# Where a pair's split weights begin in their tile: byte 88 in place of byte 8

## The chip, the cores and the metric

The kernel runs on one core of a Trainium2 chip. Its metric is the device time of one execution in microseconds. Five engines work side by side: TensorE multiplies matrices (PE in the profile; PEld is its load of the stationary operand, which overlaps the matmuls), VectorE (DVE), ScalarE (ACT) and GpSimd (POOL) work on elements, and SyncE (SP) only starts transfers. Operands of TensorE lie in SBUF, 128 partitions with a run of bytes in each; results go to PSUM.

## What is computed

A trunk of two encoder layers on 512 frames of 1024 channels, in float32. Each layer has two recurrent branches behind one wide projection, a merge, a channel block and an embedding:

```python
h = rmsnorm(x, norm1_g[i])
z = h @ w_in[i] + b_in[i]
...
y_m = (jax.nn.sigmoid(mo.astype(f32)) * head_layernorm(hm, m_norm_g[i], M_HEADS)).astype(dt)
...
y_r = (jax.nn.silu(rg.astype(f32)) * head_layernorm(hr, r_norm_g[i], R_HEADS)).astype(dt)
merged = jax.nn.sigmoid(gm) * (y_m @ w_bm[i]) + jax.nn.sigmoid(gr) * (y_r @ w_br[i])
x = x + merged @ w_out[i]
h2 = rmsnorm(x, norm2_g[i])
x = x + jnp.square(jax.nn.relu(h2 @ w_ff1[i] + b_ff1[i])) @ w_ff2[i] + b_ff2[i]
h3 = rmsnorm(x, norm3_g[i])
x = x + jax.nn.sigmoid(h3 @ w_pe_gate[i]) * (p[i] @ w_pe[i])
```

Nearly all of the time goes into the products with the weight matrices.

## The kernel before

**Three products for one.** TensorE works here on float32 values that are rounded to a shorter form (`F32R`). To keep the precision, every operand is split into a high part (rounded) and a low part (the rest), and a product becomes three matmuls: high by high, high by low, low by high (`mm3`, lines 488 to 490). Activations stay in SBUF in split form. Weights arrive from memory in raw tiles (`wr`), and `prep_next` splits each raw tile into a tile `both` with `split`: ScalarE writes the high half (line 309), VectorE the low half behind it (line 310). `both` has 2w + 64 float32 per partition, where w is 1024, or 512 for the piece called D.

**Units.** The work is a fixed list of units, in the order in which TensorE runs them. The kinds that matter here:

- `T8`: one column of 128 outputs by 1024 inputs. `t8` runs 24 matmuls; the weights are stationary (128x128) and the activations move, 512 columns.
- `PAIR`: two such columns together, by a scheme that needs seven products of half-size blocks in place of eight. `run_pair` runs seven products of 12 matmuls (lines 539 to 541), again with weights stationary and activations moving, now 256 columns. The weights of a pair lie in four tiles, `w_A`, `w_B`, `w_C` (two products each) and `w_D` (one).
- `WIDE`: the same scheme for values and gates, with activations stationary and weights moving (lines 583 to 585).
- The last four `T8` units (`LAST`) have tiles in a pool of their own and run with 256 columns at a time.

Besides these, `scores` and `attend` compute the recurrences in blocks, through `mm3` as well. In `attend` the split scores `ph` and `pl` are stationary and the split values `vh` and `vl` move; in branch A there are 258 columns, which start at column (h % 2) x 258 of the value tile for head h.

**Order.** Weights are prepared two pieces ahead of TensorE (`LOOK`), loads run on SyncE's queue in the order of the units with four raw tiles at a time, and `in_order` keeps splits and loads in that order. Sums of weight blocks that the seven-product scheme needs are made in memory by transfers on GpSimd's queue, at a pace set by the matmuls (line 367).

**Where operands start.** Tiles are placed one after another in a partition, and `o` in `prep_next` shifts the split weights inside their tile: by 2 float32 (8 bytes) for pairs and for the last four units, by none for the others. The two halves start at `o` and `o + w`; stationary blocks are 128 float32 (512 bytes) long, moving blocks 256 or 512 float32.

Of the kernel before, what the change touches and what calls it, by code (L numbers as in the profile page):

```python
# [124 lines left out]
def is_wide(g):  # L125
    return g[1][:2] in ("rv", "rw")
# [7 lines left out]
def has_t2(g):  # L134

    return is_full(g) or g[1][0] == "f"
# [117 lines left out]
def build(ctx, tc, ins, out):  # L254
    nc = tc.nc
    ve, ac, gp, te = nc.vector, nc.scalar, nc.gpsimd, nc.tensor
    units = [u for i in range(L) for u in unit_list(i)]
    NU = len(units)

    def pool(name, bufs, **kw):  # L260
        return ctx.enter_context(tc.tile_pool(name=name, bufs=bufs, **kw))
# [8 lines left out]
    wpool = pool("w", PIECES)  # L270
# [31 lines left out]
    def ps(name):  # L302
        return psum.tile([P, T], F32, name=name, tag="ps")
# [4 lines left out]
    def split(src, hi_ap, lo_ap):  # L308
        a = ac.activation(hi_ap, src, AF.Copy)  # L309
        return a, ve.tensor_sub(lo_ap, src, hi_ap.bitcast(F32))  # L310

    def in_order(kind, *new):

        for a, b in zip(cur.get(kind, ()), new):
            tc.add_manual_dep(b.ins, a.ins.name, ORDER, reason="order of the weights")
        cur[kind] = new
# [4 lines left out]
    for g, v in groups().items():  # L321
        index[g] = len(index)
        src, n, w = ("wwide", 2, UN) if is_wide(g) else ("wpairs", len(v), Q)
# [63 lines left out]
    def full(n):  # L387
        return units[n][0] in ("PAIR", "WIDE") and is_full(units[n][1])
# [10 lines left out]
    def halves(n):  # L399

        return [slice(0, Q), slice(Q, UN)] if n == 1 else [slice(0, UN)]

    def fill_raws(most=RAWS + 1):
        while at["load"] < len(loads) and len(raws) + len(kept) < most:
            n, x = loads[at["load"]]
            r = None
            if n in cur["room"] and cur["more"] not in raws:
                cur["more"] = n, x
                r = cur["low"].tile([P, UN], F32, name=f"wr{at['load']}", tag="wrx", bufs=1)
            elif len(raws) - (cur["more"] in raws) >= RAWS:  # L410
                break
            raws[n, x] = r = r or wpool.tile([P, UN], F32, name=f"wr{at['load']}", tag="wr", bufs=RAWS)
            if x:
                _, g, p = units[n]
                assert made.get((g, x[1] if is_wide(g) else p)) == 2 * len(MADE_OF(g)), (g, p, made, at["unit"])
                if is_wide(g):
                    in_order("load", nc.sync.dma_start(r, block(g, x[0])[x[1]]))
                else:
                    for k, y in enumerate(PIECE[x][:1] if x == "B" and not has_t2(g) else PIECE[x]):
                        in_order("load", nc.sync.dma_start(r[:, k * Q:(k + 1) * Q], block(g, y)[p]))  # L420
            elif units[n][0] == "IF":
                eng = nc.sync if n else nc.scalar
                eng.dma_start(r[:, 0:64], ins["wif"][n * L // NU])
            else:
                w = ins["wstream"][at["whole"]]
                for c in halves(n):
                    in_order("load", nc.sync.dma_start(r[:, c], w[:, c]))
                at["whole"] += 1
            at["load"] += 1

    def prep_next():
        n, x = order[at["prep"]]
        at["prep"] += 1
        fill_raws()

        w = Q if x == "D" else UN
        pl = cur["last"] if n >= NU - LAST else wpool
        kw = {"tag": "d", "bufs": 1} if x == "D" else {"tag": "l", "bufs": LAST} if pl is not wpool else {
            "tag": "w", "bufs": PIECES}
        wide = isinstance(x, tuple)  # L440
        nm = f"{x[0]}{x[1]}" if wide else x
        gates = units[n][0] == "IF"
        both = pl.tile([P, 2 * w + SLACK], F32R, name=f"w{n}_{nm}", **kw)
        o = 2 if units[n][0] == "PAIR" or pl is not wpool else 0
        out_ = [both[:, o + a * w:o + a * w + w] for a in range(1 if gates else 2)]
        r = formed.pop((n, x), None)
        if r is None:
            r = raws.pop((n, x))
        if gates:
            z = out_[0]  # L450
            gp.memset(z.bitcast(F32), 0.0)
            z = z.rearrange("p (k g c) -> p k g c", g=4, c=32)
            split(r[:, 0:64].rearrange("p (k g c) -> p k g c", g=2, c=H), z[:, :, 0:2, 0:H], z[:, :, 2:4, 0:H])
        elif x == 0:
            with tc.high_priority(AHEAD if n < 10 and units[n][0] == "V" or units[n][1:] == SOON else 0):
                for c in halves(n):
                    in_order("prep", *split(r[:, c], *[a[:, c] for a in out_]))
        else:
            in_order("prep", *split(r[:, :w], *out_))
        pieces[n, x] = out_  # L460
        if full(n) or not wide and x in ("A", "C") and has_t2(units[n][1]):
            pass
        elif x == "A" or wide and x[0] == "t2":
            kept[n, x] = r
        elif x == "C":

            ve.tensor_tensor(raws[n, "B"][:, Q:], kept.pop((n, "A"))[:, Q:], r[:, :Q], OP.add)
        elif x == "B":

            ve.tensor_tensor(r[:, :Q], r[:, :Q], r[:, Q:], OP.add)  # L470
            formed[n, "D"] = r
        elif wide and x[0] == "B21":
            t = cur["br"].tile([P, UN], F32, name=f"t4{n}_{x[1]}", tag=("ph", "pl")[x[1]])
            ve.tensor_tensor(t, kept.pop((n, ("t2", x[1]))), r, OP.add)
            formed[n, ("t4", x[1])] = t

    def ready(k):
        while at["prep"] < min(len(order), k + 1):
            prep_next()
# [12 lines left out]
    def t8(act, name):  # L492

        _, wh, wl = unit("T8")
        o = ps(name)
        for k in range(KT):
            s = slice(k * P, (k + 1) * P)
            mm3(o, wh[:, s], wl[:, s], act[0][k], act[1][k], k == 0, k == KT - 1)
            if k == 3:
                flush()  # L500
            if k in (2, 5):
                pace()
        return o
# [482 lines left out]
    for i in range(L):  # L986
# [322 lines left out]
        for d in range(4):  # L1309
            o = t8(xa, f"l{i}m0z{d}") if d else oz  # L1310
# [115 lines left out]
        for c in range(KT):  # L1426
# [6 lines left out]
            o = t8(yr, f"l{i}br1{c}")  # L1433
# [37 lines left out]
        for c in range(KT):  # L1471
            o = t8((mh, ml), f"l{i}wo{c}")
# [144 lines left out]
        for c in range(KT - LAST if last else KT):  # L1617
            o = t8(n3.act, f"l{i}pg{c}")
# [44 lines left out]
    for a, n in enumerate(nn):  # L1663
        for c in range(KT - LAST, KT):
            _, wh, wl = ws[c - KT + LAST]
            o = ps(f"pl{a}{c}")[:, :256]
# [141 lines left out]
```

## Time and profile before

| | |
|---|---|
| runs shown | 2291.69, 2293.63 and 2295.32 us, median 2293.63 |
| profiled execution | 2292.93 us, its span 2291.2 us |
| mean granted TensorE clock | 0.998 |
| instructions | 36395, of them 13532 matmuls |
| memory read and written | 478.03 MB and 194.51 MB |

The span runs from the first to the last instruction; the rest of an execution's time lies around it. A row of the timeline gives start, duration, engine, line, operation, the tiles as out<-in, and partitions x elements of the operand that moves. Ends of matmuls are modelled, and neighbours overlap, so what a matmul costs in a stream of them is the step from one start to the next. Names leave out buffer numbers: `l0r0brqa<-l0xnh,w_A` is a matmul from a pair's tile A and the high activations into the PSUM tile `a`.

### The profile page before, as it was taken

Reading aid. Unit: us, or ns where it says so; the run is one execution under the profiler, and the core shown is the slowest. Engines: PE = TensorE matmul, PEld = TensorE weight load, DVE = VectorE, ACT = ScalarE, POOL = GpSimd, SP = SyncE. Lnnn points to the kernel's source line nnn. Section 1 sums busy time; section 2 is a strip of 40 time slices with the busy share of each in tenths; the row PEclk is TensorE's granted clock in tenths of the full one; section 3 lists DMA queues with packets and bytes.
Section 4 is the critical chain, followed back from the end, with each engine's and each line's share of the span. In section 5 each row is a group of like instructions: output and inputs, shape, how many; then the busy total and the mean of one; then the engine's idle time right before and its main releaser. Section 6 shows DMA issues by size and latency. Waiting matters only on the chain.

```text
span 2291.2 us, 36395 instructions
## 1 busy us (share of the span) xinstructions
PE 2273.9 (99%) x13532; PEld 2019.5 (88%) x13532; DVE 1761.7 (77%) x2722; ACT 1266.5 (55%) x1835; POOL 607.7 (27%) x952
## 2 busy tenths in 40 slices
PE   9999999999999999999999999999999999999998
PEld 7888899888898899999888888988888988999997
DVE  7877767886767878778778787778868678787785
ACT  6756544654554546556557564445545546566564
POOL 3332222223124322223432332221221242111112
PEclk9999999999999999999999999999999999999999
DMA  6776887787788888888786768877877898878751
GB/s 215 192 191 174 244 232 218 216 236 220 220 247 260 216 230 234 232 245 214 222 225 184 195 178 250 235 215 223 229 217 214 248 263 221 247 236 230 229 161 56
DMA packets 187890, 499.33 MB, mean 218 GB/s; under 512 B 26352, under 2 KB 29808, under 8 KB 187712
## 3 DMA queue, kind: packets, MB, share of 16 engines
q0 software_dynamic: 57520, 188.53, 36.7%
q1 hardware_dynamic: 114496, 280.97, 36.3%
q10 hardware_dynamic: 15696, 27.50, 3.6%
q8 instruction: 106, 1.74, 0.3%
q14 instruction: 72, 0.59, 0.1%
HBM read 478.03 MB, written 194.51 MB: 294 GB/s over the span
## 4 chain that ended last, share of the span: by engine, by line
PE 88%; DVE 6%; ACT 2%; issue 2%; DMA 2%; POOL 0%; DVEq 0%; SPq 0%; ACTq 0%; POOLq 0%
PE l0f L488 1%; PE l0f L489 1%; PE l0f L490 1%; PE l1br L488 1%; PE l0br L488 1%; PE l0br L490 1%; PE l1br L490 1%; PE l1br L489 1%; PE l0br L489 1%; PE l1f L488 1%; PE l1f L490 1%; PE l1f L489 1%; DVE w_B L310 1%; PE l0pg L488 1%; PE l0pg L490 1%
## 5 line engine op out<-in xcount | busy, mean ns | idle before, releaser
L309 ACT ACTIVATE w<-wr 128x1024 fp32r<-128x1024 f32 (+1 forms) x193 | 199.7, 1041 | 125.4 <-issue 28.5
L310 DVE TENSOR_TENSOR w<-wr,w 128x1024 fp32r<-128x1024 f32 (+1 forms) x193 | 234.1, 1216 | 44.5 <-ACT w L309 43.7
L309 ACT ACTIVATE w_B<-wr 128x1024 fp32r<-128x1024 f32 x123 | 130.4, 1060 | 150.3 <-PE l0bm L490 13.1
L310 DVE TENSOR_TENSOR w_B<-wr,w_B 128x1024 fp32r<-128x1024 f32 x123 | 150.2, 1222 | 53.5 <-ACT w_B L309 53.0
L309 ACT ACTIVATE w_C<-wr 128x1024 fp32r<-128x1024 f32 x75 | 79.3, 1057 | 65.4 <-issue 9.3
L310 DVE TENSOR_TENSOR w_C<-wr,w_C 128x1024 fp32r<-128x1024 f32 x75 | 92.5, 1233 | 26.2 <-ACT w_C L309 22.5
L309 ACT ACTIVATE w_A<-wr 128x1024 fp32r<-128x1024 f32 x75 | 79.1, 1054 | 42.5 <-PE l1bm L490 4.4
L310 DVE TENSOR_TENSOR w_A<-wr,w_A 128x1024 fp32r<-128x1024 f32 x75 | 91.7, 1223 | 13.7 <-ACT w_A L309 11.1
L309 ACT ACTIVATE w_t<-wr 128x1024 fp32r<-128x1024 f32 x56 | 59.4, 1061 | 63.4 <-PE l1g2va L585 6.3
L309 ACT ACTIVATE w_D<-wr 128x512 fp32r<-128x512 f32 x75 | 47.3, 631 | 82.7 <-DVE wr L470 27.1
L310 DVE TENSOR_TENSOR w_t<-wr,w_t 128x1024 fp32r<-128x1024 f32 x56 | 68.2, 1222 | 21.0 <-ACT w_t L309 20.4
L488 PE MATMUL l0f<-l0n2h,w 128*128 128x512 f32 x176 | 68.7, 390 | 0.0
L490 PE MATMUL l0f<-l0n2h,w 128*128 128x512 f32 x176 | 68.5, 389 | 0.0
L489 PE MATMUL l0f<-l0n2l,w 128*128 128x512 f32 x176 | 68.5, 389 | 0.0
L310 DVE TENSOR_TENSOR w_D<-wr,w_D 128x512 fp32r<-128x512 f32 x75 | 51.7, 690 | 15.3 <-ACT w_D L309 14.8
L367 POOL DMA_DIRECT2D s30t<-wpairs x24 | 16.9, 703 | 91.9 <-PE l1o11a L541 9.2
L490 PEld LDWEIGHTS l0f<-l0n2h,w 128*128 128x128 f32 x176 | 33.0, 188 | 7.0
L488 PEld LDWEIGHTS l0f<-l0n2h,w 128*128 128x128 f32 x176 | 33.0, 188 | 6.5
L489 PEld LDWEIGHTS l0f<-l0n2l,w 128*128 128x128 f32 x176 | 33.0, 188 | 6.4
L488 PE MATMUL l1f<-l1n2h,w 128*128 128x512 f32 x96 | 37.5, 391 | 0.0
L490 PE MATMUL l1f<-l1n2h,w 128*128 128x512 f32 x96 | 37.4, 390 | 0.0
L489 PE MATMUL l1f<-l1n2l,w 128*128 128x512 f32 x96 | 37.4, 389 | 0.0
(5796 smaller groups left out, 9080.8 us busy)
## 6 DMA issues: line engine op xcount, KB each, us to landing
wr<-wstream SPq DMA_DIRECT2D x189, 512.0 KB, 4.8
wr<-wpairs SPq DMA_DIRECT2D x225, 256.0 KB, 4.1
wr<-wwide SPq DMA_DIRECT2D x48, 512.0 KB, 4.7
s3t<-wwide POOLq DMA_DIRECT2D x24, 256.0 KB, 4.3
s6t<-wwide POOLq DMA_DIRECT2D x24, 256.0 KB, 5.2
s18t<-wwide POOLq DMA_DIRECT2D x24, 256.0 KB, 5.1
s21t<-wwide POOLq DMA_DIRECT2D x24, 256.0 KB, 5.1
s24t<-wpairs POOLq DMA_DIRECT2D x24, 256.0 KB, 5.7
```

Source lines behind the costliest of these rows:

```text
L309: a = ac.activation(hi_ap, src, AF.Copy)
L310: return a, ve.tensor_sub(lo_ap, src, hi_ap.bitcast(F32))
L367: dma = gp.dma_start(piece(g, x, p, q), piece(g, MADE[x][a], p, q), max_dma_last_dim=4096, **kw)
L488: te.matmul(o, sh, mh, start=first, stop=False)
L489: te.matmul(o, sh, ml, start=False, stop=False)
L490: cur["mm"] = te.matmul(o, sl, mh, start=False, stop=last)
```

## The change

One line of `prep_next`. For pairs `o` becomes 22 float32 in place of 2, so both halves of `w_A`, `w_B`, `w_C` and `w_D` begin 80 bytes further into their tile, at byte 88. The last four units keep 2 and all others 0. The tile sizes stay: 22 + 2w fits in 2w + 64. Counted modulo 256 bytes, a pair's moving operand starts 168 bytes past its stationary one, where it was 248.

```diff
         both = pl.tile([P, 2 * w + SLACK], F32R, name=f"w{n}_{nm}", **kw)
-        o = 2 if units[n][0] == "PAIR" or pl is not wpool else 0
+        o = 22 if units[n][0] == "PAIR" else 2 if pl is not wpool else 0
         out_ = [both[:, o + a * w:o + a * w + w] for a in range(1 if gates else 2)]
```

## The prediction

> **What bounds the kernel now.** First the page, parts 1 and 4: how busy each engine is, and which engine the chain of work that ended last runs through.
>
> ```profile
> PE 2273.9 (99%) x13532; PEld 2019.5 (88%) x13532; DVE 1761.7 (77%) x2722; ACT 1266.5 (55%) x1835; POOL 607.7 (27%) x952
> PE 88%; DVE 6%; ACT 2%; issue 2%; DMA 2%; POOL 0%; DVEq 0%; SPq 0%; ACTq 0%; POOLq 0%
> PEclk9999999999999999999999999999999999999999
> ```
>
> TensorE is busy 99% of the span and carries 88% of the chain, at full granted clock in every slice. So the time is, to first order, the sum over the matmuls of the step from one start to the next; I call that step the pitch. Busy durations do not show it, because neighbouring matmuls overlap. The timeline does. Second view, therefore: the timeline of TensorE in a run of pairs.
>
> ```profile
> 304.20 0.28 PE L541 MATMUL l0r0brqa<-l0xnh,w_A 128*128 128x256 f32 x1
> 304.32 0.28 PE L539 MATMUL l0r0brqa<-l0xnh,w_A 128*128 128x256 f32 x1
> 304.43 0.28 PE L540 MATMUL l0r0brqa<-l0xnl,w_A 128*128 128x256 f32 x1
> ...
> 308.94 0.28 PE L540 MATMUL l0r0brqb<-l0xnl,w_B 128*128 128x256 f32 x1
> ```
>
> From 304.20 to 308.94 lie 41 steps: 4.74 / 41 = 115.6 ns of pitch for a pair's matmul with 256 moving columns, across three products and two weight tiles. The full-width matmuls of `t8`, 512 columns, in the same view, 30 steps apart:
>
> ```profile
> 289.68 0.39 PE L488 MATMUL l0bm<-l0ymh,w 128*128 128x512 f32 x1
> ...
> 296.48 0.39 PE L488 MATMUL l0bm<-l0ymh,w 128*128 128x512 f32 x1
> ```
>
> 6.80 / 30 = 226.7 ns. How many matmuls the change touches, from the view of busy time in two stretches for line L539 alone:
>
> ```profile
> 0.00:1145.00 1145.00, 274.24 (x980) 183.88 (x980) 1.00 0.79 223
> 1145.00:2291.00 1146.00, 313.06 (x1120) 210.25 (x1120) 1.00 0.75 213
> ```
>
> That is 2100 on L539. L540 and L541 issue once for each of them, so there are 6300: 6300 x 115.6 ns = 728 us, a third of the span. **One nanosecond of pitch is worth 6.3 us.**
>
> **What the change moves.** No instruction is added, removed or reordered; no DMA, queue or wait changes. Two addresses in each pair tile move 80 bytes up. Tiles that hold operands are a whole number of 256-byte steps long per partition (512 floats, 2w + 64, 576, 1280), so I count leads, moving start minus stationary start, modulo 256: 248 before and 168 after, for all 6300.
>
> *Writes.* ScalarE and VectorE write the halves at the new place. Groups of part 5, tiles at byte 8 (`w_A`, `w_C`) against tiles at byte 0 (`w_t`), the same shape:
>
> ```profile
> L309 ACT ACTIVATE w_C<-wr 128x1024 fp32r<-128x1024 f32 x75 | 79.3, 1057 | 65.4 <-issue 9.3
> L310 DVE TENSOR_TENSOR w_C<-wr,w_C 128x1024 fp32r<-128x1024 f32 x75 | 92.5, 1233 | 26.2 <-ACT w_C L309 22.5
> L309 ACT ACTIVATE w_t<-wr 128x1024 fp32r<-128x1024 f32 x56 | 59.4, 1061 | 63.4 <-PE l1g2va L585 6.3
> L310 DVE TENSOR_TENSOR w_t<-wr,w_t 128x1024 fp32r<-128x1024 f32 x56 | 68.2, 1222 | 21.0 <-ACT w_t L309 20.4
> ```
>
> 1057 against 1061 ns and 1233 against 1222: the starting byte costs at most 11 ns of a write, either way, and both engines have room (below). I cost it at nothing.
>
> *Reads.* While a matmul streams its moving columns, the load of the next stationary block reads the same memory; the lead says how far apart the two start. Does the trace show that leads matter? `m_attend` has matmuls of 258 columns with two leads: values start at byte 0 of their tile for even heads and at 258 x 4 = 1032, which is 8 modulo 256, for odd ones; the stationary tile is not shifted. The timeline of head 0 (lead 0; the last row is the first matmul after its 30) and of head 1 (lead 8, 29 steps):
>
> ```profile
> 94.12 0.28 PE L488 MATMUL l0m0a<-l0m0vh,l0m0ph 128*128 128x258 f32 x1
> ...
> 97.72 0.40 PE L488 MATMUL l0m0o<-l0n1h,w 128*128 128x512 f32 x1
> ```
>
> ```profile
> 140.84 0.28 PE L488 MATMUL l0m1a<-l0m0vh,l0m1ph 128*128 128x258 f32 x1
> ...
> 144.28 0.28 PE L490 MATMUL l0m1a<-l0m0vh,l0m1pl 128*128 128x258 f32 x1
> ```
>
> 3.60 / 30 = 120.0 ns at lead 0 and 3.44 / 29 = 118.6 ns at lead 8. So the pitch does depend on the lead. The price of a column follows from two widths at the same lead 0: (226.7 - 120.0) / (512 - 258) = 0.42 ns. Taken to 256 columns: 119.2 ns at lead 0, 117.8 at lead 8, 115.6 at lead 248. 256 columns at 0.42 ns with nothing lost would be 107.5 ns. What a matmul pays above its columns is therefore 11.7, 10.3 and 8.1 ns for those leads.
>
> [...]
>
> *The unknown term* is the pitch at lead 168, which nothing in the trace has. Its ends: 107.5 ns (nothing lost), 8.1 x 6.3 = 51 us gained; and lead 0's 119.2 ns, 3.6 x 6.3 = 23 us lost. I take this value: all three leads seen lie within 8 bytes of 0, and the step from 0 to 248 took away 3.6 of 11.7 ns, 31%. Going ten times as far from 0, I let it take that share once more of the 8.1 that are left: 2.5 ns, a pitch of 113.1. It is nearest to the pair's own row. 6300 x 2.5 ns = 15.8 us.
>
> *What lies beside it, and what is late next.* The view of busy time by stretch, two stretches that are nearly all pairs (columns: length, then busy time of PE, PEld, DVE, ACT and POOL, clock, DMA share, GB/s):
>
> ```profile
> 496.00:515.00 19.00, 19.00 (x126) 17.35 (x125) 17.43 (x26) 8.76 (x15) 3.61 (x6) 1.00 0.81 237
> 905.00:954.00 49.00, 49.00 (x387) 47.42 (x386) 36.85 (x58) 23.08 (x29) 10.94 (x17) 1.00 0.87 248
> ```
>
> VectorE fills 17.43 of 19 us (92%) in the first and 75% in the second; DMA 81 and 87%. A pair stage 2.2% shorter (2.5 of 115.6) puts these at 94% and 89%: still under TensorE. But TensorE does wait for others at the edges of pairs; the view of line L539 says for whom, in us and times:
>
> ```profile
>   DVE l1x L1532: 5.4, 12
>   DVE l0x L1532: 1.9, 5
> ```
>
> Time saved just before such a wait comes back as a longer wait. These are 17 waits in 75 pairs, and the fullest stretch above has 8% to spare; I take one part in ten as lost, with none and a quarter as its ends. Gain: 15.8 x 0.9 = 14.2 us.
>
> **The sum** is made against the profiled execution, 2292.9 us with a span of 2291.2; the median of the runs shown is 2293.6, so the same to 0.03%. 2292.9 - 14.2 = 2278.7, say **2279 us**.
>
> **The rivals.**
>
> *No effect.* The lead counts only while both streams start on the same bytes; 248 is already clear of that and 168 is too. For it: of the 11.7 ns at lead 0, most (8.1) is still there at 248, so much of it may be a fixed price of changing the stationary block. Against it: lead 8 is as far from 0 as 248 and pays 10.3, not 8.1, so more than touching starts is at work. Time: 2292.9, or 2288.4 to 2297.5 within 0.7 ns of pitch. [...]
>
> *Slower: the overtaking moves into the run.* The moving stream reads 256 columns while the load reads 128, so it gains on the load by 512 bytes. If the two collide whenever the difference passes a multiple of 256, lead 248 collides 8 bytes after the start and once in the middle; lead 168 after 88 bytes and after 344, both in full flow. For it: lead 8, whose passings come late in the run (248 and 504 bytes on), has the dearer pitch. Against it: lead 0 is the dearest of all and has a passing at its start. Price: lead 8's pitch, 117.8, is 2.2 ns more, 13.9 us: 2307 us; at lead 0's 119.2 it is 2316. It decides against the change once the pitch is over 116.3 ns (0.7 x 6.3 = 4.6 us, 0.2%).
>
> *VectorE takes over.* If the pitch fell all the way to 107.5 ns, 7%, stretches such as 496 to 515 would be bound by VectorE (92%) and a good part of 51 us would stay out: about 2250 us rather than 2242. It ends on the same side as the forecast.
>
> **How the numbers follow.** Forecast, lower pitch: 0.48, with its own range 2255 to 2288 (pitch 108.9 to 114.7, nine tenths of the gain counted); the full fall to VectorE's bound is the low tail of this, 0.05. No effect: 0.22. Overtaking inside the run: 0.30, at 2298 to 2316. The bound of 0.2%, 4.6 us, is about what a measurement of this kernel tells from no change; so faster 0.48, within it 0.22, slower 0.30. Below 2260 I put 0.08 and above 2313 0.06; the range that leaves these out is 2260 to 2313.
>
> **What would show it.** In the trace after: the pitch in a run of pairs from the timeline, 113 (forecast), 115.6 (no effect), 118 or more (overtaking). The same in the durations of L539 to L541: now 277 ns at a pitch of 115.6, against 283 at 120.0 in these rows of lines L540 and L489:
>
> ```profile
> L540 PE MATMUL l0r0brqc<-l0xsl,w_A x4: 277/277/278, 305.5 to 306.5; 128*128 128x256 f32 x4
> L489 PE MATMUL l0m0a<-l0m0vl,l0m0ph 128*128 128x258 f32 x10 | 2.8, 283 | 0.0
> ```
>
> Lower pitch should bring about 275 ns, no effect 277, overtaking 279 or more. The 512-column groups (226.7 ns of pitch) must stay, since their tiles do not move. ACT and DVE groups on `w_A` to `w_D` should keep their means; if they grow by tens of ns, the write was not free. The forecast is wrong if the pitch falls and the span does not follow by nine tenths of it, or if the pitch rises. Least certain is the share of 31%, which rests on two leads that sit side by side.

## The result, and the profile after

The change makes the kernel faster by two parts in a thousand: 2288.66 us against 2292.83 us on the same chip (medians of 12 runs each), a ratio of 0.998 with a 95% interval of 0.9973 to 0.9987. That is 4.2 us; the forecast was 14 us. The direction held, the size was over three times too large.

The profiled execution after has a span of 2286.3 us, 4.9 us less than before, at the same mean granted clock of 0.998. Parts 1 and 4 of its page, busy time by engine and the shares of the chain that ended last:

```profile
PE 2266.4 (99%) x13532; PEld 2011.6 (88%) x13532; DVE 1761.6 (77%) x2722; ACT 1265.9 (55%) x1835; POOL 610.0 (27%) x952
PE 87%; DVE 7%; ACT 2%; issue 2%; DMA 2%; POOL 0%; SPq 0%; DVEq 0%; ACTq 0%; POOLq 0%
```

TensorE still bounds the kernel, but one point of the chain has gone from PE to DVE: that is the first sign that something was given back. The pitch itself is in the timeline. Two places in it, after the change:

```profile
368.88 0.28 PE L490 MATMUL l0r0s<-l0r0qh,l0r0kl 128*128 128x256 f32 x1
369.00 0.28 PE L539 MATMUL l0r1brqa<-l0xnh,w_A 128*128 128x256 f32 x1
...
373.55 0.28 PE L539 MATMUL l0r1brqb<-l0xnh,w_B 128*128 128x256 f32 x1
...
910.85 0.28 PE L539 MATMUL l0o11c<-l0hh,w_C 128*128 128x256 f32 x1
...
914.59 0.28 PE L539 MATMUL l0o12c<-l0hh,w_A 128*128 128x256 f32 x1
```

From 369.00 to 373.55 lie 39 steps, 116.7 ns each; from 910.85 to 914.59 lie 33, 113.3 ns each. Both stretches have the same lead of 168 bytes, the same kind of tile and the same instructions. Before the change all pairs ran at one pitch (115.6 ns in the prediction's rows); now there are mainly two, one below it and one above, and a pair that runs at one of them mostly does so from end to end.

Two more views of after. First the same two stretches of L539 as in the prediction (length, busy time and count of PE and PEld, clock, DMA share, GB/s):

```profile
0.00:1145.00 1145.00, 272.51 (x980) 183.90 (x980) 1.00 0.80 224
1145.00:2287.00 1142.00, 311.55 (x1120) 210.25 (x1120) 1.00 0.75 213
```

A matmul of L539 lasts 278 ns on average (272.51 / 980), 1.8 ns less than the 280 of before. Second, the groups of the splits and of the full-width matmuls (part 5 of the page):

```profile
L309 ACT ACTIVATE w_C<-wr 128x1024 fp32r<-128x1024 f32 x75 | 79.3, 1058 | 65.0 <-issue 6.8
L310 DVE TENSOR_TENSOR w_C<-wr,w_C 128x1024 fp32r<-128x1024 f32 x75 | 92.5, 1233 | 25.6 <-ACT w_C L309 24.7
L488 PE MATMUL l0f<-l0n2h,w 128*128 128x512 f32 x176 | 68.7, 390 | 0.0
```

The writes at byte 88 take 1058 and 1233 ns, where they took 1057 and 1233 at byte 8. The 512-column group has the same 390 ns in both pages.

Last, who TensorE waits for (view of waits; line waited for: us in total, times, longest). Before:

```profile
PE l1o20a L539 <- DVE l1x L1532: 0.8, 1, 0.8
PE l0o10a L539 <- DVE l0x L1532: 0.5, 1, 0.5
...
PE l1o10a L540 <- DVE l1hl L310: 0.3, 1, 0.3
...
PE l1f10a L541 <- DVE w_B L310: 0.3, 1, 0.3
```

After:

```profile
PE l1o20a L539 <- DVE l1x L1532: 1.2, 1, 1.2
...
PE l1f10a L541 <- DVE w_B L310: 0.8, 1, 0.8
PE l0o10a L539 <- DVE l0x L1532: 0.7, 1, 0.7
...
PE l1o10a L540 <- DVE l1hl L310: 0.6, 1, 0.6
```

The same four waits, all for VectorE, each longer by 0.2 to 0.5 us.

**The bookkeeping for all pairs.** I took the start of every matmul on L539 to L541 from the timeline and formed the step from each to the next matmul. A step of up to 130 ns counts as pitch. Of a longer one, what lies above 115.7 ns counts as a wait.

| | before | after | difference |
|---|---|---|---|
| mean pitch, ns | 115.71 | 114.22 | -1.49 |
| waits in the pairs, us | 12.9 | 16.8 | +3.9 |
| all steps together, us | 741.9 | 736.5 | -5.4 |
| span, us | 2291.2 | 2286.3 | -4.9 |

Over some 6230 steps the pitch gives 9.3 us, the waits take 3.9 back, and the 5.4 that are left are the span's 4.9 to half a microsecond. Of the 3.9 us, 2.9 lie in long steps whose idle time the profile ends with VectorE (8.3 us before, 11.1 after) and 0.9 in such that end with ScalarE (0.3 and 1.2). The other large groups did not move: the steps of all 512-column matmuls on L488 to L490, most of them `T8`, add up to 1006.2 and 1006.1 us, those of the wide units to 305.4 and 305.5. So all of the result lies in the pairs, and two things are to be explained: why the pitch is 114.2 and not less, and why only 58% of its gain arrives.

### The profile page after: what moved, and what is told of

It reads as the page before. It is cut to its first block, busy times and chain, and to the rows that moved or that the text cites. A ratio compares the mean times of both kernels' runs of the same rounds, so it can differ in the third digit from the quotient of the medians.

```text
span 2286.3 us, 36395 instructions
## 1 busy us (share of the span) xinstructions
PE 2266.4 (99%) x13532; PEld 2011.6 (88%) x13532; DVE 1761.6 (77%) x2722; ACT 1265.9 (55%) x1835; POOL 610.0 (27%) x952
## 4 chain that ended last, share of the span: by engine, by line
PE 87%; DVE 7%; ACT 2%; issue 2%; DMA 2%; POOL 0%; SPq 0%; DVEq 0%; ACTq 0%; POOLq 0%
PE l1br L488 1%; PE l0br L489 1%; PE l0br L488 1%; PE l1br L489 1%; PE l0br L490 1%; PE l1br L490 1%; PE l0f L488 1%; PE l0f L490 1%; PE l0f L489 1%; DVE w_B L310 1%; DVE w_C L310 1%; PE l1f L488 1%; PE l0pg L488 1%; PE l1f L490 1%; PE l1bm L488 1%
## 5 line engine op out<-in xcount | busy, mean ns | idle before, releaser
L310 DVE TENSOR_TENSOR w<-wr,w 128x1024 fp32r<-128x1024 f32 (+1 forms) x193 | 234.1, 1216 | 43.7 <-ACT w L309 42.8
L310 DVE TENSOR_TENSOR w_B<-wr,w_B 128x1024 fp32r<-128x1024 f32 x123 | 150.2, 1222 | 54.3 <-ACT w_B L309 53.8
L309 ACT ACTIVATE w_C<-wr 128x1024 fp32r<-128x1024 f32 x75 | 79.3, 1058 | 65.0 <-issue 6.8
L310 DVE TENSOR_TENSOR w_C<-wr,w_C 128x1024 fp32r<-128x1024 f32 x75 | 92.5, 1233 | 25.6 <-ACT w_C L309 24.7
L310 DVE TENSOR_TENSOR w_A<-wr,w_A 128x1024 fp32r<-128x1024 f32 x75 | 91.7, 1223 | 13.7 <-ACT w_A L309 9.6
L310 DVE TENSOR_TENSOR w_t<-wr,w_t 128x1024 fp32r<-128x1024 f32 x56 | 68.3, 1222 | 21.3 <-ACT w_t L309 20.7
L488 PE MATMUL l0f<-l0n2h,w 128*128 128x512 f32 x176 | 68.7, 390 | 0.0
L490 PE MATMUL l0f<-l0n2h,w 128*128 128x512 f32 x176 | 68.5, 389 | 0.0
L310 DVE TENSOR_TENSOR w_D<-wr,w_D 128x512 fp32r<-128x512 f32 x75 | 51.7, 690 | 15.0 <-ACT w_D L309 14.5
L367 POOL DMA_DIRECT2D s30t<-wpairs x24 | 16.8, 701 | 92.3 <-PE l1o10a L541 9.2
L490 PEld LDWEIGHTS l0f<-l0n2h,w 128*128 128x128 f32 x176 | 33.0, 188 | 7.0
L488 PEld LDWEIGHTS l0f<-l0n2h,w 128*128 128x128 f32 x176 | 33.0, 188 | 6.6
L488 PE MATMUL l1f<-l1n2h,w 128*128 128x512 f32 x96 | 37.6, 391 | 0.0
L490 PE MATMUL l1f<-l1n2h,w 128*128 128x512 f32 x96 | 37.4, 389 | 0.0
```

Of the source, the lines that this page charges most:

```text
L367: dma = gp.dma_start(piece(g, x, p, q), piece(g, MADE[x][a], p, q), max_dma_last_dim=4096, **kw)
L488: te.matmul(o, sh, mh, start=first, stop=False)
L490: cur["mm"] = te.matmul(o, sl, mh, start=False, stop=last)
```

## The experiments

Three questions: is it the lead at all, and which rule does it follow; what decides between the two steady pitches; and who takes the rest back. Unless said otherwise, each kernel is the changed one with the edit shown. "Pairs" below is the sum of the steps as in the table, 741.9 us before and 736.5 after.

### Is it the lead? Four other places

```diff
-        o = 22 if units[n][0] == "PAIR" else 2 if pl is not wpool else 0
+        o = 0 if units[n][0] == "PAIR" else 2 if pl is not wpool else 0
```

That is lead 0; with 20, 34 and 16 in place of 0 the halves begin at bytes 80, 136 and 64 and the leads are 176, 120 and 192. Lead 176 is 8 bytes from the change's 168; 120 is nearly as far from 0, counted modulo 256, as a lead can be.

> Pairs' halves at byte 0 of their tiles, lead 0; nothing else differs from the kernel before. Theory 'the lead sets the pitch': the pairs' matmuls step at about 119 to 120 ns, as the 258-column matmuls at lead 0 do, so 3.5 to 4.3 ns more than before, 22 to 27 us slower than before (2315 to 2320 us). Theory 'the lead has no price of its own and 168 only changed how stretches begin': 115.7 ns and 2293 us.

> [...] Theory 'distance from lead 0 sets the pitch': the same as at 168, a most frequent step of 113 to 114 ns, some 2288 us. [...]

> [...] Theory 'the farther from 0 the cheaper': 113 ns or less, 2288 us or below. Theory 'both streams collide whenever the moving one has gained a multiple of 256 bytes, wherever that falls': the same two passings as at 168, so the same mean of 114.2 ns, 2288 us. Theory 'single leads are good or bad by how the two streams fall in step': any value from 110 to 120 ns, not ordered by distance.

> Pairs' halves at byte 64, lead 192, the only other lead of the map whose mean was under 115 ns (114.85, at 113 and 114 for two thirds of its steps, in two to three pairs). Theory 'single leads are good, 168 and 192 alike': most pairs step at 113.3 ns, 2287 to 2290 us. Theory 'the map's few pairs were lucky in what ran before them': a mean of 116 ns or more, 2296 us or more.

| lead | time, us | before on the same chip | mean pitch, ns | pairs, us | waits in them, us |
|---|---|---|---|---|---|
| 0 | 2314.49 (one run) | 2292.63 | 119.9 | 762.8 | 7.6 |
| 176 | 2306.88 (one run) | 2292.63 | 118.7 | 755.8 | 8.2 |
| 120 | 2306.19 (one run) | 2292.63 | 118.0 | 752.2 | 9.1 |
| 192 | 2295.3 (10 runs) | 2293.02 | 116.5 | 745.1 | 11.6 |

Lead 192 has a ratio of 1.0011 (1.0001 to 1.002). The pitch in a run of pairs, from the timelines of leads 0, 176, 120 and 192 in this order:

```profile
308.19 0.28 PE L539 MATMUL l0r0brqb<-l0xnh,w_B 128*128 128x256 f32 x1
...
312.87 0.28 PE L539 MATMUL l0r0brka<-l0xnh,w_A 128*128 128x256 f32 x1
```

```profile
308.22 0.28 PE L539 MATMUL l0r0brqb<-l0xnh,w_B 128*128 128x256 f32 x1
...
312.85 0.28 PE L539 MATMUL l0r0brka<-l0xnh,w_A 128*128 128x256 f32 x1
```

```profile
308.27 0.28 PE L539 MATMUL l0r0brqa<-l0xsh,w_B 128*128 128x256 f32 x1
...
312.87 0.28 PE L539 MATMUL l0r0brka<-l0xnh,w_A 128*128 128x256 f32 x1
```

```profile
308.72 0.28 PE L539 MATMUL l0r0brqb<-l0xnh,w_B 128*128 128x256 f32 x1
...
312.96 0.28 PE L539 MATMUL l0r0brka<-l0xnh,w_A 128*128 128x256 f32 x1
```

39 steps in 4.68 us are 120.0 ns; 39 in 4.63 are 118.7; 39 in 4.60 are 117.9; 36 in 4.24 are 117.8. So where the weights start in their tile does set the pitch, and "no effect" falls: lead 0 costs 20.9 us more in the pairs than lead 248, and 21.9 in the time. The prediction's price for lead 0, worked out from 258 columns, was 119.2, and 119.9 was measured.

The 119.9 ns of lead 0 and the 114.2 of lead 168 come from the same instructions with the pairs' weights in another place. What inside the chip makes the difference, no run shows.

What falls as well is every simple order. The rule of distance says that 120, nearly half way round, is best of all: it has 118.0. The rule of passings, the slower rival's, puts 120, 168, 176 and 192 on one footing, with two passings inside the run: they have 118.0, 114.2, 118.7 and 116.5. And 168 and 176 are 8 bytes apart.

### All leads in one kernel

Each pair unit, each `T8` unit and each wide tile takes the next of 32 places, 8 bytes apart.

```diff
+    def scan(n, x, pl):
+        k = units[n][0]
+        if k not in ("PAIR", "T8", "WIDE"):
+            return 0
+        if k == "PAIR":
+            return scans.setdefault(n, 2 * (sum(u[0] == k for u in units[:n]) % 32))
+        return scans.setdefault((n, x), 2 * (sum(1 for a, b in order[:place[n, x]] if units[a][0] == k) % 32))
...
-        o = 22 if units[n][0] == "PAIR" else 2 if pl is not wpool else 0
+        o = scan(n, x, pl)
```

> A map in one run: from the kernel before, each pair, each full-width unit and each wide tile gets a start of its own, bytes 0, 8, 16 and so on to 248 in turn (pairs and full-width units: leads 0, 248, 240 down to 8; wide tiles, whose weights move: leads 0, 8 and so on to 248). Read is the mean step by lead, not the time. [...] For 512 columns: if what helps one width hurts the other, as lead 168 did (233.3 against 226.7), 226.7 is at or near the least of its map; otherwise some leads lie at 220 ns or less, 34 us on 5100 matmuls.

Its time, 2330.61 us (one run, 2292.16 before), is not the point. The mean steps by lead are, without the first six matmuls of each unit:

| | pairs, 256 columns | `T8`, 512 columns |
|---|---|---|
| lead 0 | 119.9 | 227.7 |
| lead 120 | 118.0 | 233.3 |
| lead 136 | 118.0 | 226.7 |
| lead 168 | 114.9 | 233.3 |
| lead 176 | 118.9 | 232.1 |
| lead 192 | 114.9 | 233.4 |
| lead 248 | 115.6 | 230.6 |
| all 32 | 114.9 to 120 | 226.7 to 234.1 |

Of 32 leads only 168, 192 and 248 give pairs a mean below 116 ns. They are single teeth: the neighbours of 168 and 192 (160, 176, 184, 200) have 117.3 to 118.9. Nor are odd multiples of 8 ordered apart from even ones: 168 and 248 are odd and 192 is even, while 120 and 136, odd, and 176, even, are slow (118.0, 118.0 and 118.9 ns). For 512 columns the good leads are others: 0 and 136 (227.7 and 226.7 ns).

The wide tiles of the same run show one thing more, for there the weights move and the stationary activations keep their place. Without the first three matmuls of each tile, their mean step goes from 228.3 ns at lead 0 to 234.5 at lead 136 and 235.9 at lead 120. So the stationary start by itself does not decide, at 512 columns at least. Nor does the lead, counted modulo 256, by itself: at lead 136 all five `T8` units run at 226.6 to 226.7 ns and all three wide tiles at 234.5.

Each lead was seen in two or three pairs only, and lead 192 was better here than in a kernel of its own; the next but one section says how that can be.

### Is 168 good for other shapes? `T8` at the same lead

```diff
-        o = 22 if units[n][0] == "PAIR" else 2 if pl is not wpool else 0
+        o = 22 if units[n][0] in ("PAIR", "T8") else 0
```

> The change, and in addition the stationary weights of all full-width units (512 moving columns, now at lead 0) 88 bytes into their tiles, lead 168. Theory 'the lead costs a matmul what the two streams lose together, whatever its width': the 512-column step falls from 226.7 by what pairs gain from lead 0 to 168, some 6 ns, on some 5100 matmuls: 30 us, down to about 2258 us. Theory 'a 512-column matmul has time to hide it, since the load takes only half of it': the step stays at 226.7 ns and the time within 2 us of the change's, 2288 us.

2310.84 us (4 runs) against 2292.63, a ratio of 1.0076 (1.0059 to 1.0092). In its timeline, 30 steps of `T8`:

```profile
290.90 0.39 PE L488 MATMUL l0bm<-l0ymh,w 128*128 128x512 f32 x1
...
297.90 0.39 PE L488 MATMUL l0bm<-l0ymh,w 128*128 128x512 f32 x1
```

7.00 / 30 = 233.3 ns, against 226.7 before. That is neither theory: the step did not fall and did not stay, it rose. All 512-column steps on L488 to L490 add up to 1030.1 us, 24.0 more than with the change alone, while the pairs stay at 737.2. The edit also moves the weights of the last four units, which run with 256 columns, from byte 8 to byte 88, and their mean step falls from 115.7 to 113.8 ns. So in one kernel the lead that helps 256 columns hurts 512, and of the 32 places scanned none is among the best for both.

### Two pitches at one lead: which pairs are slow?

The changed kernel once more, with a profile of its own:

> The changed kernel itself, for a second profile of it and as the measure for the three beside it. Both theories: 2287 to 2290 us. Theory 'two steady steps': every pair again steps at 113.3 or 116.7 ns; the eight behind the scores at 116.7 again; pairs behind a long wait (heads of branch A's channel block) may swap, so the mean lies between 113.9 and 114.5 ns. Theory 'fixed by the tiles': the same pairs as before are slow, all of them.

2289.21 us (10 runs), ratio 0.9982 (0.9973 to 0.9991), pairs 737.3 us: the same result. Its mean pitch is 114.54 ns and its waits are 15.6 us, so here the pitch gives 7.3 us and the waits take 2.7 back; how the gain splits differs from one execution to the next. Nor are the slow pairs the same. In after, eleven of the 75 pairs run at 116.5 to 116.7 ns: the query and key pairs of branch r of heads 1 and 3 in both layers (`l0r1brq`, `l0r1brk`, `l0r3brq` and so on, eight), and `l1o12`, `l1o13` and `l1f21`. Three more change their step in the middle (`l0bgm2`, `l1o11` and `l0o33`). In this second profile the eight are slow again, but `l1o12` and its neighbours run at 113.3, and `l0o01` to `l0o03`, `l0o21` to `l0o23`, `l0f11` and `l0f31` are slow. The view of tile `l0o02a` (duration least/median/most in ns, first and last start), after:

```profile
L539 PE MATMUL l0o02a<-l0hh,w_A x4: 276/276/276, 832.4 to 833.4; 128*128 128x256 f32 x4
...
L539 PE MATMUL l0o02a<-l0hh,w_C x4: 276/276/276, 840.5 to 841.5; 128*128 128x256 f32 x4
```

and in the second profile of the same kernel:

```profile
L539 PE MATMUL l0o02a<-l0hh,w_A x4: 278/280/280, 833.0 to 834.1; 128*128 128x256 f32 x4
...
L539 PE MATMUL l0o02a<-l0hh,w_C x4: 279/280/280, 841.4 to 842.5; 128*128 128x256 f32 x4
```

The same program, tile and address need 8.1 us from the first row to the second in one execution and 8.4 in another. Lead 192 does the same: in its kernel nine pairs run at 113.3 and forty at 117.8, so the scan's few pairs showed it too well. The lead does not fix the pitch alone; something else chooses. The step can even change inside a pair. The view of tile `l0o33a`, after:

```profile
L539 PE MATMUL l0o33a<-l0hh,w_A x4: 276/276/276, 1078.5 to 1079.5; 128*128 128x256 f32 x4
...
L539 PE MATMUL l0o33a<-l0hh,w_B x4: 283/283/356, 1082.8 to 1084.0; 128*128 128x256 f32 x4
...
L539 PE MATMUL l0o33a<-l0hh,w_D x4: 276/276/281, 1091.4 to 1092.4; 128*128 128x256 f32 x4
```

Its steps are 113 and 114 ns up to two long ones (146 and 194 ns, at the first matmuls of `w_B`), then 120 ns for most of the pair, then 113 and 114 again. In `l1o11` and `l0bgm2` the step goes from 113.3 to 116.7 right behind such long steps too, though many other pairs go on at 113.3 behind theirs. The eight that are slow in both profiles stand behind the scores of heads 0 and 2 (`l0r0s` at 368.88 above), the query pair first, and the scores' own 256-column matmuls run at lead 0 with steps of 117 to 121 ns.

### What decides: another matmul in front

To change what a pair follows, and nothing in the pair, I added one matmul of 512 columns behind those scores, into a PSUM tile that nothing reads:

```diff
-            return scores(f"l{i}r{h}", qk[0], qk[1], qk[2], qk[3], lambda a: dg[:, 0:T - a * P])
+            r = scores(f"l{i}r{h}", qk[0], qk[1], qk[2], qk[3], lambda a: dg[:, 0:T - a * P])
+            if h % 2 == 0:
+                te.matmul(ps(f"l{i}r{h}more"), qk[2][0][:, 0:P], qk[0][0], start=True, stop=True)
+            return r
```

A kernel with three of them (through `mm3`) went first:

> The change, and three matmuls of 512 columns more (a repeat whose result nobody reads) between the scores of heads 0 and 2 of branch B and the pairs behind them, in both layers; without them those pairs follow 256-column matmuls at lead 0, and all eight run at 116.6 ns. Theory 'lead 168 has two steady steps, and what TensorE ran just before decides which one a stretch falls into': the eight pairs now run at 113.3 ns as those behind full-width units do, 2.2 us less, against 2.7 us for the twelve added matmuls, so 2288 to 2290 us. Theory 'these pairs are slow by their own tiles or addresses': they stay at 116.6 ns and the time grows by 2.7 us.

> The change with one added 512-column matmul (not read by anybody) in place of three between the scores of heads 0 and 2 of branch B and their pairs. Theory 'what ran just before decides the step, and one matmul is enough': the eight pairs at 113.3 ns, 8 x 0.26 = 2.1 us gained and 4 x 0.23 = 0.9 us paid, 1 us less than the change. Theory 'it takes several to settle': the eight stay at 116.7 ns and the time grows by 0.9 us.

The timeline with the one added matmul, at the place of the slow stretch above:

```profile
368.53 0.28 PE L490 MATMUL l0r0s<-l0r0qh,l0r0kl 128*128 128x256 f32 x1
368.65 0.39 PE L1147 MATMUL l0r0more<-l0r0qh,l0r0kh 128*128 128x512 f32 x1
...
369.23 0.28 PE L539 MATMUL l0r1brqa<-l0xnh,w_A 128*128 128x256 f32 x1
...
373.99 0.28 PE L539 MATMUL l0r1brqb<-l0xnh,w_B 128*128 128x256 f32 x1
```

42 steps in 4.76 us: 113.3 ns. All eight pairs run at it but for a few single steps (means of 113.3 to 113.8), with one added matmul as with three. (With three, `l0o10` to `l0o13` and `l0o20` to `l0o23`, at 113.3 to 114.5 after the change, rose to between 115.9 and 116.9.) The pair's code, weights and lead are those of the change; what stands in front of it differs. That this chooses the pitch is shown for these eight. Two things come with the added matmul and were not tested apart: 0.2 us of time, and one turn of the pool of eight PSUM tiles, so that later results go to other tiles. For the pairs behind `l0o00` or `l1o11`, where no instruction differs between executions, it is only argued that a wait of another length ahead of them does the same.

The times: three added matmuls 2287.1 us (one run, 2292.16 before); one added 2288.52 us (10 runs, ratio 0.9977, 0.9967 to 0.9986). The pairs take 4.6 us less than in the changed kernel's second profile (732.7 for 737.3). Some 2 us of this are the eight pairs; the rest are others that ran at another step this time. The four added matmuls cost 0.9 us, an estimate from 227 ns each. The medians lie only 0.7 us apart and the intervals overlap, so this version is not shown to be better than the change.

### Who takes the rest back: VectorE's share removed

These two kernels leave out the low halves of the pairs' weights: the second half of the tile is not written, and the matmuls of L541 read the high half instead. The matmuls are as many and as long; VectorE has 300 instructions less. One has o = 2 (lead 248), the other o = 22 (lead 168 for L539 and L540); L541 reads the high half in both, at the same lead.

```diff
                 for c in halves(n):
                     in_order("prep", *split(r[:, c], *[a[:, c] for a in out_]))
+        elif units[n][0] == "PAIR":
+            in_order("prep", ac.activation(out_[0], r[:, :w], AF.Copy))
+            out_[1] = out_[0]
         else:
```

> The kernel before with the low halves of pairs' weights left out: TensorE reads the high half in their place, at the same lead and in the same number of matmuls, and VectorE loses some 4.3 us for each pair. Theory 'what the change gained in pitch came back as waits at the edges of pairs, because VectorE supplies weights and operands there': waits in pairs, 12.9 us over all before, fall to a few us, and this kernel is about 10 us faster than before, 2283 us. Theory 'those waits are TensorE's own results going round through PSUM': they stay near 13 us.

> The change with the same low halves left out. Theory 'waits took back the gain': against the other kernel without low halves the whole gain in pitch arrives, 1.5 ns or more on 6300 matmuls, 9 to 14 us, 2270 to 2274 us. Theory 'the gain is lost elsewhere': the difference between the two stays at 4 to 5 us, as between the change and before.

| | lead 248 | lead 168 | difference |
|---|---|---|---|
| time, us (4 runs each) | 2283.74 | 2274.78 | -8.96 |
| ratio to before | 0.9962 (0.9947 to 0.9976) | 0.9922 (0.9905 to 0.9939) | |
| mean pitch, ns | 115.63 | 114.17 | -1.46 |
| waits in the pairs, us | 1.3 | 1.4 | +0.1 |
| pairs, us | 729.8 | 720.7 | -9.1 |

Part 1 of the page for lead 168, and its view of waits (its lines stand three further down than in the change):

```profile
PE 2259.9 (99%) x13532; PEld 2008.7 (88%) x13532; DVE 1467.6 (65%) x2422; ACT 1263.8 (56%) x1835; POOL 601.8 (26%) x952
```

```profile
PE l1gr0a L542 <- DVE l1gr0y L625: 0.5, 1, 0.5
PE l0gr0a L542 <- DVE l0gr0y L625: 0.5, 1, 0.5
PE l0o33a L542 <- DVE l0x L1535: 0.5, 1, 0.5
```

With VectorE at 65% instead of 77% the waits at `l1o20a`, `l0o10a` and `l1f10a` are gone, in both. And now the same difference in pitch, 1.46 ns, arrives whole: 9.1 us in the pairs, 9.0 in the time, where the change alone brings 4.2. So it is VectorE's share of the work that keeps back the other half. (`l1o21` to `l1f31` ran at 116.7 here, `l1o12` at 113.3, and the eight pairs of branch r at 116.3 to 117.0, slow as before.)

One attempt to use this moved one subtraction of each pair's operand from VectorE to GpSimd:

```diff
-        ve.tensor_tensor(v[:, 4:6, :], v[:, 1:3, :], v[:, 0:1, :].to_broadcast([P, 2, S]), OP.subtract)
+        gp.tensor_tensor(v[:, 4:6, :], v[:, 1:3, :], v[:, 0:1, :].to_broadcast([P, 2, S]), OP.subtract)
```

> The change with one subtraction of each hidden block of the channel part (128x512) on GpSimd in place of VectorE. Theory 'the waits in pairs come from VectorE being late': with less on VectorE they fall by a few us of 16.8, and the time with them, unless GpSimd is later with its part than VectorE was. Theory 'the waits come from elsewhere': no difference, 2288 us, or slower where GpSimd takes longer.

2309.19 us (4 runs), ratio 1.0068 (1.0053 to 1.0083): a miss. Its waits:

```profile
PE l1o10a L540 <- DVE l1hl L310: 2.1, 1, 2.1
PE l1o20a L540 <- DVE l1hl L310: 2.1, 1, 2.1
...
PE l0o10a L539 <- DVE l0x L1532: 1.6, 1, 1.6
```

The subtraction stands on the way from a hidden block to the matmuls of the pairs that read it, and VectorE's split of its result (L310) comes later than before; the waits in the pairs are 31.9 us, where the changed kernel in the same batch had 15.6. These 16.3 are most of the 20.0 us by which it is slower than that kernel. It shows that the edges are paid in full, and leaves open how much less work on VectorE would be worth with the full computation.

## Where the prediction was right and where it failed

**The bound** was right: TensorE, 99% busy at a granted clock of 0.998, with the pairs a third of the span. All of the gain came from the pairs, and a nanosecond of pitch is worth 6.2 us where nothing takes it back (9.1 / 1.46).

**Writes cost nothing**: right, to 1 ns in 1057.

**The 512-column groups stay**: right, 1006.2 and 1006.1 us of steps; their tiles did not move.

**The unknown term**, "that share once more of the 8.1 that are left: 2.5 ns", is where the forecast fails first, and not in one way. The rule behind it was wrong: it made a lead better the farther it lies from 0, and lead 120 lies farther than 168 and has 118.0. That the rule landed almost on the steady value at 168 (113.1 forecast, 113.3 measured) was luck, and so was the direction: 29 of the 32 leads in the scan are dearer than 248. One of its rows was also read too finely: 118.6 ns for lead 8 comes from times rounded to 10 ns, and the 29 steps of each odd head average 119.0, those of each even head 119.8, so leads 0 and 8 lie 0.8 ns apart and not 1.4. What the step did not have is that a lead can have more than one steady pitch. Of the 14.8 us between 115.71 and 113.33 ns the eleven slow pairs keep 3.0 (11 pairs of 83 steps at 3.3 ns more), the three that change in the middle 0.7, and single longer steps below 130 ns the remaining 1.8. What is left is the 1.49 ns, 9.3 us, in place of 15.8.

**"One part in ten as lost"** was mis-sized too: 3.9 of 9.3 us, 42% (2.7 of 7.3, 37%, in the second profile), beyond even the quarter that was its far end. By the prediction's own sign, that the span must follow by nine tenths of the pitch, the forecast is wrong here. The row it rested on was right: the waits of L539 for VectorE, which after the change read

```profile
  DVE l1x L1532: 6.4, 10
  DVE l0x L1532: 2.0, 4
```

for 5.4 and 1.9 us. But the share was set by how full VectorE is in a stretch (92%), and what counts is what stands at the edge. The waits exist because a matmul of the pair needs an operand or a split of weights that VectorE finishes last, and VectorE got no faster (1761.7 us busy before, 1761.6 after). Only 1.1 of the 3.9 us shows in these two rows. By the steps of the bookkeeping, the 2.9 us for VectorE are 1.1 for the splits of `w_B`, which the prediction did not look at, 0.8 for `l1hl`, and 1.0 for `x` and the like. The stretches themselves had the room that was forecast, as the same view as in the prediction shows after the change:

```profile
496.00:515.00 19.00, 19.00 (x127) 17.28 (x126) 17.52 (x26) 8.82 (x15) 3.59 (x6) 1.00 0.85 241
905.00:954.00 49.00, 49.00 (x387) 47.09 (x386) 36.45 (x57) 23.32 (x31) 10.39 (x17) 1.00 0.88 246
```

17.52 of 19 us and 36.45 of 49 are 92% and 74%, where they were 92% and 75%.

The sum, by the forecast's own terms, is 9.3 x 0.58 = 5.4 us in place of 15.8 x 0.9 = 14.2.

**No effect** fell: lead alone moves the mean pitch between 114.2 and 119.9 ns. The measured time, 2288.66 us, lies just inside its range all the same (2288.4 to 2297.5), through what was given back and not through its mechanism.

**Overtaking inside the run** fell as stated: 120, 168, 176 and 192 have the same passings and four pitches. Its price was no invention, though: 117.8 ns is about what a lead of the scan costs on average, and a lead picked without measuring would more likely have lost than won.

**VectorE takes over** was meant for a pitch of 107.5 ns and does not hold in that form. A small version of it is what happened: VectorE is not the bound, but at the edges of pairs it holds back two fifths of a gain of 1.3% in the pitch.

**What stays open** is why 168, 192 and 248 are good for 256 columns and 0 and 136 for 512. In the pairs only the stationary operand was moved. The scan's wide tiles show for 512 columns that neither the stationary start nor the lead modulo 256 decides by itself; what does is not shown.

## What to carry to other kernels

Where TensorE's stream is the bound, the place of its operands within a tile is worth trying: here it moved a matmul's step by up to 5% (114.2 ns at lead 168, 119.9 at lead 0). But it has to be scanned for each length and measured in the whole kernel: leads 168 and 176, 8 bytes apart, differ by 4% (114.2 and 118.7 ns), and the best place for 256 columns was among the worst for 512 (lead 168: 233.3 ns, where the scan had 226.7 to 234.1). A mean pitch can hide two steady ones (114.2 ns here, mainly of 113.3 and 116.7); look at the steps unit by unit, and at what stands in front of the slow units. And count the gain only up to the next wait: where a stage begins by waiting for another engine, a faster TensorE in front waits longer for it (16.8 us in the pairs, 12.9 before), so relieve that engine first, or take the loss into the sum.

## What the runs showed of the hardware

Many of the steady values are multiples of 3.33 ns: pairs ran at 113.3, 116.7 or 120.0 ns and `T8` at 226.7 or 233.3. Others are not (115.6 at lead 248, 117.8 at lead 192, 118.0 at lead 120). Some values are means of unequal steps that repeat: the 116.7 of lead 168 is made of steps of 115 to 118 ns, the 113.3 of 113 and 114. At lead 168 a pair mostly takes 113.3 or 116.7, with one stretch at 120, and which one can be switched by a single matmul in front of it: the eight pairs of branch r went from 116.7 to 113.3 with one matmul of 512 columns put ahead, and but for a few single steps stayed there.
